# One layer step on one core: two plain FF blocks by tiles, the next weights ahead of an evaluation, staging kept, a late scaling

## The chip, the cores and the metric

The kernel runs on one NeuronCore of a Trainium2 chip. The metric is the device time of one execution in microseconds. Five engines have queues of their own and work each in its own order: TensorE (PE, matmuls and transposes), VectorE (DVE), ScalarE (ACT), GpSimd (POOL) and SyncE (SP, which issues the DMAs).

## What is computed

One layer of a streaming encoder, in fp32, for 512 prompt tokens and 8 sequences of 16 new tokens, each with 512 tokens in caches. Of the reference the parts that the change touches:

```python
def softmax_attend(q, k, v, bias):
    scale = q.shape[-1] ** -0.5
    s = jnp.einsum('bqhd,bkhd->bhqk', q, k).astype(jnp.float32) * scale + bias
    p = jax.nn.softmax(s, axis=-1).astype(v.dtype)
    return jnp.einsum('bhqk,bkhd->bqhd', p, v)
...
def layer_tail(x, ada, o_a, o_b, gates, w_o_a, w_o_b, w_out, g_norm_ffn, w_gate, w_up, w_down):
    shift1, scale1, gate1, shift2, scale2, gate2 = ada
    B, S = o_a.shape[:2]
    y_a = o_a.reshape(B, S, N_HEADS_A * V_DIM_A) @ w_o_a
    y_b = o_b.reshape(B, S, N_HEADS_B * HEAD_DIM_B) @ w_o_b
    x = x + gate1 * ((gates[:, :, 0] * y_a + gates[:, :, 1] * y_b) @ w_out)
    h = modulate(rmsnorm(x, g_norm_ffn), shift2, scale2)
    return x + gate2 * ((jax.nn.silu(h @ w_gate) * (h @ w_up)) @ w_down)
```

D_MODEL is 1024, D_FF 2816 (22 blocks of 128). Ahead of this stand the adaLN terms, an input projection, a latent attention (MLA) and a band attention, for the prompt and for the samples.

## The kernel before

Every fp32 operand is split in two parts of a shorter type, a high part (a cast on ACT, line 86) and a low part (a subtraction on DVE, line 87). A product is three matmuls into the same bank: high by high (L94), high by low of the activations (L95), low of the weights by high (L96). PSUM has two groups of four banks, tiles named mm and tr. The tokens are five tiles of 128: four of the prompt, one of the samples.

The program runs through stages. Ahead of 473 us: norms, projections, prompt attention. To 582: a loop over the 8 sample sequences. The softmax of the band scores divides by its sum with a `tensor_scalar` on DVE (L682); the probabilities are transposed on PE (L140) and multiplied by the cached values (L1003), and ACT copies the result to o2 (L1007). Then the latent values are projected up (L1070, to 585.74), and ACT copies them out (L1075) and casts them to `oh`, the high part of the attention outputs. Then w_o in four quarters of columns, to 657, w_out in two halves, to 714.7, and the feed-forward part.

Weights come by DMA into raw tiles of 128 x 1024 and are split from there. Up to the value projection the raw tiles are those of a pool wstA (3 of w_raw, 3 each of w_hi and w_lo, 1024 wide). Then that pool is closed, and a pool wops takes its place: 4 raw tiles and operands of 512 columns, 12 high (op_hi) and 11 low (op_lo).

The first two feed-forward blocks are plain: gate and up products of h with a block's weights, each over tiles 0 to 2 (384 columns) and tiles 3 and 4 (256). They run while the last tiles are still being made: h2_cols normalizes, transposes (xn to tr, L140) and modulates a tile's columns into hfull, and splits them into hB. Blocks 2 to 21 use seven products instead of eight halves, with sums of weight quarters made on POOL and DVE (`sums`, one buffer) and sums of h (hsum, hS). One of these, hB's fourth (fourth_sum), is made on DVE from hB and hS, and uses the buffer of `sums` too. The copies of partial products (u) that this needs are on ACT (L1293). Each engine's order is set by the order in which the program issues instructions, moved by a scheduler that runs ahead of the chip.

Of the kernel before, what the change touches and what calls it, by code (L numbers as in the profile page):

```python
# [17 lines left out]
P = 128  # L18
# [30 lines left out]
def layer_kernel(  # L49
# [117 lines left out]
    wa_cm = pool("wstA", side="right")  # L167
    wa = wa_cm.__enter__()

    raws = [3]  # L170

    def load_raw(src, shape, rows=P, given=P):
        n = shape[0] * shape[1]
        raw = wa.tile([P, 1024], F32, tag="w_raw", bufs=raws[0], name=nm("wraw"))[:rows, :n]
        rv = raw.rearrange("p (k n) -> p k n", k=shape[0])
        if given < rows:
            G.memset(raw, 0.0)
        nc.sync.dma_start(rv[:given], src)
        return raw, rv

    def load_kv_up(c0):
        raw = wa.tile([P, 1024], F32, tag="w_raw", bufs=raws[0], name=nm("wraw"))
        for k in range(2):
            nc.sync.dma_start(raw[:, k * 512:(k + 1) * 512].rearrange("p (h c) -> p h c", c=64),
                              wkv_v[:, k, :, c0:c0 + 64])
        return raw
# [491 lines left out]
    def softmax_rows(pl, src, nmax, w, dst, eng):  # L678
        sm = pl.tile([P, 1], F32, tag="sm", bufs=4, name=nm("sm"))
        S.activation(out=dst[:, :w], in_=src, func=AF.Exp, bias=nmax, accum_out=sm)  # L680
        V.reciprocal(sm, sm)
        eng.tensor_scalar(out=dst[:, :w], in0=dst[:, :w], scalar1=sm, scalar2=None, op0=ALU.mult)  # L682
# [153 lines left out]
    with pool("ework") as ew:  # L836
# [34 lines left out]
        def softmax(s, sc, mx):  # L871
            nmax = et([P, 1], "nmax", 4)
            V.tensor_reduce(out=nmax, in_=mx, op=ALU.max, axis=AX.X, negate=True)
            pr = et([P, KEYS], "Pr", 2)
            softmax_rows(ew, sc, nmax, KEYS, pr, V)
            pn = et([P, P], "Pn", 2)
            G.memset(pn, 0.0)
            G.tensor_copy(pn[:, s * DSEQ:(s + 1) * DSEQ], pr[:, PAST:])
            return pr, pn
# [101 lines left out]
        def band_softmax(st):  # L981
            sc, mx = et([P, KEYS], "S", 2), et([P, 2], "mx", 4)
            for hf in range(2):
                ks = slice(hf * KH, (hf + 1) * KH)
                V.tensor_tensor_reduce(out=sc[:, ks], in0=st["ps"][hf][:, :KH], in1=biasd[:, ::-1][:, ks], scale=1.0,
                                       scalar=-3e38, op0=ALU.add, op1=ALU.max, accum_out=mx[:, hf:hf + 1])
            st["P"] = softmax(st["s"], sc, mx)
# [6 lines left out]
        def band_values(st, half):  # L994
# [10 lines left out]
            if half:  # L1005
                st["o2"] = et([P, P], "o2", 2)
                S.copy(st["o2"], st["po"][:, :P])  # L1007
# [72 lines left out]
    wa_cm.__exit__(None, None, None)  # L1080

    wa = ctx.enter_context(pool("wops", side="right"))
    raws[0] = 4

    def operand(src, n=512):
        hi = wa.tile([P, 512], F32R, tag="op_hi", bufs=12, name=nm("ophi"))[:, :n]
        lo = wa.tile([P, 512], F32R, tag="op_lo", bufs=11, name=nm("oplo"))[:, :n]
        split(hi, lo, src)
        return hi, lo

    def operands(src, shape):
        raw = load_raw(src, shape)[0]
# [9 lines left out]
    def ada_rows(c0):  # L1102
        raw = wa.tile([P, 1024], F32, tag="w_raw", bufs=4, name=nm("wraw"))
# [4 lines left out]
    def gate_rows(c0, scale):  # L1108
# [3 lines left out]
        for c in range(2):  # L1112
            hi = wa.tile([P, 512], F32R, tag="op_hi", bufs=12, name=nm("ophi"))[0:AR, :]
            lo = wa.tile([P, 512], F32R, tag="op_lo", bufs=11, name=nm("oplo"))[0:AR, :]
# [116 lines left out]
    def ff_raw(fb):  # L1231
        cs_ = slice(fb * P, (fb + 1) * P)
        return [load_raw(v[:, :, cs_], [KD, P])[0] for v in (wg_v, wu_v)]
# [24 lines left out]
    def plain(bank, w, t0, t1):  # L1258
        for k in range(KD):
            ks = slice(k % 4 * P, (k % 4 + 1) * P)  # L1260
            h = [x[:, k // 4 * 2:k // 4 * 2 + 2, k % 4, t0 * 64:t1 * 64] for x in hB]
            mm3(bank[:, :(t1 - t0) * P].rearrange("p (a x) -> p a x", a=2), w[k // 4][0][:, ks], w[k // 4][1][:, ks],
                h[0], h[1], k == 0, k == KD - 1)

    w0 = operands_of(0)
    banks0 = [mm_tile() for _ in range(4)]
    plain(banks0[0], w0[0], 0, 3)
    h2_cols(4)
    plain(banks0[1], w0[1], 0, 3)
    plain(banks0[2], w0[0], 3, 5)  # L1270
    plain(banks0[3], w0[1], 3, 5)
# [11 lines left out]
    with pool("fwork") as fw:  # L1283
# [25 lines left out]
        def plain_block(banks0):  # L1309
            new_hidden()  # L1310
            for i, (t0, t1) in enumerate(((0, 3), (3, 5))):
                n = (t1 - t0) * P
                u = fw.tile([P, 512], F32, tag="tmp", bufs=2, name=nm("u"))[:, :n]
                S.activation(out=u, in_=banks0[2 * i][:, :n], func=AF.Silu)
                V.tensor_tensor(out=u, in0=banks0[2 * i + 1][:, :n], in1=u, op=ALU.mult)
# [22 lines left out]
        def ff_block(fb):  # L1338

            new_hidden()  # L1340
# [7 lines left out]
            G.tensor_tensor(out=s4, in0=a12, in1=a11, op=ALU.subtract)  # L1348
            pa, pb, pc = mm_tile(), tr_tile(), tr_tile()
            product(pa, o11, hB, 0)  # L1350
            u1 = part(pa, "u1", 2)
            product(pb, operand(s1), hS, 0)
# [38 lines left out]
        plain_block(banks0)  # L1391
        w1 = operands_of(1)
        banks1 = [tr_tile() for _ in range(4)]
        for i, (t0, t1) in enumerate(((0, 3), (3, 5))):
            for j in range(2):
                plain(banks1[2 * i + j], w1[j], t0, t1)
        plain_block(banks1)
        fourth_sum()
        ends = [0, 5, 10, 14, 18]
        for fb in range(2, NFF):  # L1400
            ff_block(fb)
# [60 lines left out]
```

## Time and profile before

| what | value |
|---|---|
| median of three runs | 1174.38 us (1174.12 to 1176.02) |
| the profiled execution | 1172.05 us, its span 1170.3 us |
| granted clock of TensorE, mean | 0.986 |
| PE busy | 1113.9 us, 95% of the span, 7187 matmuls |
| DVE, ACT, POOL busy | 737.1, 560.3, 214.1 us |

The span is what the trace covers; the 1.75 us around it are start and end. The times of the trace count from the start of the span.

### The profile page before, as it was taken

The page shows a single profiled execution, that of the slowest core. Times are in us where ns is not written, and L with a number is a line of the kernel's source. Part 1 is how long each engine was busy: PE and PEld are TensorE (multiplying, and loading weights), DVE is VectorE, ACT ScalarE, POOL GpSimd, SP SyncE. Part 2 cuts the span into 40 slices and gives each one's busy share as a digit, 9 for nine tenths or more (in the row PEclk, how much of TensorE's full clock was granted, in tenths as well). Part 3 has the DMA queues.
Part 4 walks back from the last instruction along what each step waited for, and adds up shares of the span by engine and source line. Part 5 has one row for each costly group of instructions (what it writes and reads, how often), then busy time and mean ns, then how long its engine had stood idle before and what let it go on. Part 6 is the DMA issues. An engine that isn't in the chain of part 4 may idle for free. (4 is left out here: it accounts for less than half of the span.)

```text
span 1170.3 us, 19416 instructions
## 1 busy us (share of the span) xinstructions
PE 1113.9 (95%) x7187; PEld 998.9 (85%) x7187; DVE 737.1 (63%) x1675; ACT 560.3 (48%) x1243; POOL 214.1 (18%) x289
## 2 busy tenths in 40 slices
PE   7898999999999999899879998899999999999998
PEld 6678988999897788798779987889899899899896
DVE  3688555747776654455456347786676677675744
ACT  4675533446665544466543246465155245253440
POOL 0010001010000000112012213243143233242320
PEclk9999999999999899999989998999999999999999
DMA  8832334587665445766496221034133223133112
GB/s 266 296 112 71 109 141 127 171 231 206 201 183 167 129 145 160 236 214 228 133 288 219 88 73 52 1 109 126 37 92 104 76 73 108 37 108 90 54 56 90
DMA packets 156425, 158.17 MB, mean 135 GB/s; under 512 B 24826, under 2 KB 115495, under 8 KB 156330
## 3 DMA queue, kind: packets, MB, share of 16 engines
q1 hardware_dynamic: 156330, 156.92, 43.5%
q8 instruction: 57, 0.93, 0.3%
q14 instruction: 38, 0.31, 0.1%
HBM read 136.59 MB, written 20.30 MB: 134 GB/s over the span
## 5 line engine op out<-in xcount | busy, mean ns | idle before, releaser
L86 ACT CAST ophi<-wraw 128x512 fp32r<-128x512 f32 (+1 forms) x188 | 113.7, 620 | 135.1 <-PE mm L96 52.8
L87 DVE TENSOR_TENSOR oplo<-wraw,ophi 128x512 fp32r<-128x512 f32 (+1 forms) x188 | 148.2, 805 | 37.5 <-ACT ophi L86 13.3
L94 PE MATMUL mm<-ophi,aT 128*128 128x512 f32 x220 | 87.1, 396 | 0.4 <-DVE u L1335 0.3
L95 PE MATMUL mm<-oplo,aT 128*128 128x512 f32 x220 | 86.9, 395 | 0.0
L96 PE MATMUL mm<-ophi,aTl 128*128 128x512 f32 x220 | 86.1, 395 | 0.0
L94 PE MATMUL mm<-hT_hi,whi 128*128 128x320 f32 x256 | 83.2, 325 | 1.5 <-ACT whi L86 1.5
L94 PE MATMUL mm<-whi,hT_hi 128*128 128x512 f32 (+3 forms) x240 | 79.5, 332 | 1.2 <-ACT jk L337 0.9
L96 PE MATMUL mm<-hT_hi,wlo 128*128 128x320 f32 x256 | 80.4, 314 | 0.0
L95 PE MATMUL mm<-hT_lo,whi 128*128 128x320 f32 x256 | 79.7, 311 | 0.0
L96 PE MATMUL mm<-whi,hT_lo 128*128 128x512 f32 (+3 forms) x240 | 79.4, 332 | 0.0
L95 PE MATMUL mm<-wlo,hT_hi 128*128 128x512 f32 (+3 forms) x240 | 79.3, 331 | 0.0
L94 PE MATMUL mm<-hB,ophi 128*128 128x320 f32 (+2 forms) x192 | 60.2, 316 | 4.6 <-ACT hB L86 4.6
L1386 DVE TENSOR_TENSOR tmp<-mm,gate 128x512 f32<-128x512 f32 x50 | 34.2, 688 | 43.4 <-PE mm L96 43.3
L95 PE MATMUL mm<-hB,ophi 128*128 128x320 f32 (+2 forms) x192 | 60.1, 314 | 0.5 <-DVE hB L87 0.5
L96 PE MATMUL mm<-hB,oplo 128*128 128x320 f32 (+2 forms) x192 | 59.9, 312 | 0.0
L94 PE MATMUL tr<-hB,ophi 128*128 128x320 f32 (+2 forms) x192 | 59.2, 309 | 0.0
L95 PE MATMUL tr<-hB,ophi 128*128 128x320 f32 (+2 forms) x192 | 59.2, 309 | 0.0
L87 DVE TENSOR_TENSOR wlo<-wraw,whi 128x1024 fp32r<-128x1024 f32 (+2 forms) x36 | 41.0, 1141 | 28.0 <-ACT whi L86 27.1
L96 PE MATMUL tr<-hB,oplo 128*128 128x320 f32 (+2 forms) x192 | 58.6, 309 | 0.0
L94 PEld LDWEIGHTS mm<-hT_hi,whi 128*128 128x128 f32 x256 | 48.7, 190 | 5.4 <-issue 2.1
L94 PE MATMUL mm<-hS,ophi 128*128 128x320 f32 x160 | 49.6, 310 | 3.3 <-ACT u L1293 3.3
L1344 POOL TENSOR_TENSOR sums<-wraw 128x512 f32<-128x512 f32 x20 | 28.3, 1416 | 130.3 <-DMA wraw<-in_w_up_dram 89.6
(374 smaller groups left out, 3272.8 us busy)
## 6 DMA issues: line engine op xcount, KB each, us to landing
adaw<-in_w_ada_dram SPq DMA_DIRECT2D x48, 512.0 KB
wraw<-in_w_in_dram SPq DMA_DIRECT2D x28, 512.0 KB
wraw<-in_w_gate_dram SPq DMA_DIRECT2D x22, 512.0 KB
wraw<-in_w_up_dram SPq DMA_DIRECT2D x22, 512.0 KB
wraw<-in_w_down_dram SPq DMA_DIRECT2D x20, 512.0 KB
lat<-in_cache_kv_latent_dram SPq DMA_DIRECT2D x16, 512.0 KB
wraw<-in_cache_band_v_dram SPq DMA_DIRECT2D x16, 512.0 KB
kn<-in_cache_band_k_dram SPq DMA_DIRECT2D x16, 512.0 KB
```

The source lines that it names most:

```text
L86: S.copy(hi, src)
L87: (eng or V).tensor_tensor(out=lo, in0=src, in1=f(hi), op=ALU.subtract)
L94: T.matmul(out, lh, rh, start=start, stop=False, skip_group_check=more)
L95: T.matmul(out, lh, rl, start=False, stop=False, skip_group_check=more)
L96: T.matmul(out, ll, rh, start=False, stop=stop, skip_group_check=more)
L1344: G.tensor_tensor(out=s1, in0=a21, in1=a22, op=ALU.add)
L1386: V.tensor_tensor(out=tmp, in0=banks[t], in1=gate2[t // 4][:, cc], op=ALU.mult)
```

## The change

Five edits. (1) The pool wstA stays open to the end. A smaller pool wops (1 raw tile, 6 high, 5 low) is opened beside it; operands are taken in turns of four, two as the halves of a w_hi/w_lo pair, two from wops, and every fourth raw tile comes from wops. The numbers stay 4 raw, 12 high, 11 low. (2) The plain blocks are taken together: tiles 0 and 1 of block 0 and of block 1 (256 columns, gate and up in one bank), then tiles 2 to 4 of both (384 columns). (3) The first steps of a seven-product block (loads, sums of quarters, the operands of the first two products) become a function of their own, ff_weights, and that of block 2 is called ahead of the evaluation of the plain blocks and of fourth_sum. (4) For the samples' band attention the probabilities are no longer scaled; the copy of o2 scales by 1/sum instead. (5) Weights that fill whole rows are loaded by a shorter function.

```diff
-    wa_cm = pool("wstA", side="right")
-    wa = wa_cm.__enter__()
-    raws = [3]
+    wa = ctx.enter_context(pool("wstA", side="right"))
...
-    def softmax_rows(pl, src, nmax, w, dst, eng):
+    def softmax_rows(pl, src, nmax, w, dst, eng, scaled=True):
         sm = pl.tile([P, 1], F32, tag="sm", bufs=4, name=nm("sm"))
         S.activation(out=dst[:, :w], in_=src, func=AF.Exp, bias=nmax, accum_out=sm)
         V.reciprocal(sm, sm)
+        if not scaled:
+            return sm
         eng.tensor_scalar(out=dst[:, :w], in0=dst[:, :w], scalar1=sm, scalar2=None, op0=ALU.mult)
...
-                S.copy(st["o2"], st["po"][:, :P])
+                S.activation(out=st["o2"], in_=st["po"][:, :P], func=AF.Copy, scale=st["sm"])
...
-    wa_cm.__exit__(None, None, None)
-
-    wa = ctx.enter_context(pool("wops", side="right"))
-    raws[0] = 4
+    wo2 = ctx.enter_context(pool("wops", side="right"))
+    turn, pair = [0, 0], [None, None]
+
+    def new_operand():
+        i, turn[0] = turn[0] % 4, turn[0] + 1
+        if i == 0:
+            pair[:] = [wa.tile([P, 1024], F32R, tag=tag, bufs=3, name=nm(tag)) for tag in ("w_hi", "w_lo")]
+        if i < 2:
+            return [o[:, i * 512:(i + 1) * 512] for o in pair]
+        return [wo2.tile([P, 512], F32R, tag=tag, bufs=n, name=nm(tag)) for tag, n in (("op_hi", 6), ("op_lo", 5))]
+
+    def new_raw():
+        i, turn[1] = turn[1] % 4, turn[1] + 1
+        return (wo2 if i == 2 else wa).tile([P, 1024], F32, tag="w_raw", bufs=1 if i == 2 else 3, name=nm("wraw"))
...
-    w0 = operands_of(0)
-    banks0 = [mm_tile() for _ in range(4)]
-    plain(banks0[0], w0[0], 0, 3)
-    h2_cols(4)
-    plain(banks0[1], w0[1], 0, 3)
-    plain(banks0[2], w0[0], 3, 5)
-    plain(banks0[3], w0[1], 3, 5)
+    w01 = [operands_of(0), operands_of(1)]
+    sums01 = []
+    for i in range(2):
+        bank = mm_tile()
+        sums01.append([[bank[:, 0:256], bank[:, 256:512]]])
+        for j in range(2):
+            plain(sums01[i][0][j], w01[i][j], 0, 2)
+        if i == 0:
+            h2_cols(4)
+    for i in range(2):
+        sums01[i].append([(tr_tile if i else mm_tile)()[:, :384] for _ in range(2)])
+        for j in range(2):
+            plain(sums01[i][1][j], w01[i][j], 2, 5)
...
-        def ff_block(fb):
-
-            new_hidden()
+        def ff_weights(fb):
             a11, a12, a21, a22 = quarters(fb)
             sums = fw.tile([P, 2, 512], F32, tag="sums", name=nm("sums"))
...
+            return a11, a12, a21, a22, s1, s4, o11, operand(s1)
+
+        def ff_block(fb, w):
+
+            a11, a12, a21, a22, s1, s4, o11, o1 = w
+            new_hidden()
...
-        plain_block(banks0)
-        w1 = operands_of(1)
-        banks1 = [tr_tile() for _ in range(4)]
-        for i, (t0, t1) in enumerate(((0, 3), (3, 5))):
-            for j in range(2):
-                plain(banks1[2 * i + j], w1[j], t0, t1)
-        plain_block(banks1)
+        first = ff_weights(2)
+        plain_block(sums01[0])
+        plain_block(sums01[1])
         fourth_sum()
         ends = [0, 5, 10, 14, 18]
         for fb in range(2, NFF):
-            ff_block(fb)
+            ff_block(fb, first if fb == 2 else ff_weights(fb))
```

What the change moves shows in the order of instructions on three engines. First SP's queue around the value projection (in_w_kv_up) and the first loads of w_o (in_w_o_a, in_w_o_b), before:

```order
L178 DMA wraw_7418<-in_cache_band_v_dram 128x2x512
L184 DMA wraw_7460<-in_w_kv_up_dram 128x8x64
L222 DMA ada_d<-adar_7404 105x512
L184 DMA wraw_7460<-in_w_kv_up_dram 128x8x64
L1147 DMA g_7569<-gate_d 128x640
L1147 DMA g_7571<-gate_d 128x640
L1147 DMA g_7639<-gate_d 128x640
L1147 DMA g_7641<-gate_d 128x640
L178 DMA wraw_7549<-in_w_o_a_dram 128x4x256
L178 DMA wraw_7559<-in_w_o_b_dram 128x4x256
```

And now:

```order
L175 DMA wraw_7400<-in_cache_band_v_dram 128x2x512
L175 DMA wraw_7410<-in_cache_band_v_dram 128x2x512
L181 DMA wraw_7452<-in_w_kv_up_dram 128x8x64
L219 DMA ada_d<-adar_7396 105x512
L181 DMA wraw_7452<-in_w_kv_up_dram 128x8x64
L1104 DMA wraw_7540<-in_w_o_a_dram 128x4x256
L1104 DMA wraw_7548<-in_w_o_b_dram 128x4x256
L1162 DMA g_7558<-gate_d 128x640
L1162 DMA g_7560<-gate_d 128x640
```

The two loads of w_o stood behind four loads of g, and stand ahead of them now; the loads of w_o use the raw slots that the band values (wraw_7400, wraw_7410) had.

Second PE in the plain blocks. The products of hB (hB_8262 or hB_8243 the high part, hB_8263 or hB_8244 the low part) with a block's weights stand around the transposes of the normalized tiles 3 and 4 (xn). Before, the transposes of tile 3 and then of tile 4, in block 0's products of tiles 0 to 2:

```order
L96 MATMUL mm_8832<-hB_8262,oplo_8821 128x384
L140 MATMUL tr_8768<-ident,xn_8741 128x128 x4
L140 MATMUL tr_8780<-ident,xn_8741 128x128 x4
L94 MATMUL mm_8832<-hB_8262,ophi_8820 128x384
...
L140 MATMUL tr_8860<-ident,xn_8810 128x128 x4
L140 MATMUL tr_8870<-ident,xn_8810 128x128 x4
L94 MATMUL mm_8833<-hB_8262,ophi_8824 128x384
```

Now, in the products of tiles 0 and 1 of block 1 (mm_8893); 70 matmuls stand ahead of the first, 14 between the two, and 12 behind the second. The last five rows begin the products of tiles 2 to 4:

```order
L94 MATMUL mm_8893<-hB_8243,op_hi_8811 128x256
L140 MATMUL tr_8741<-ident,xn_8714 128x128 x4
L140 MATMUL tr_8753<-ident,xn_8714 128x128 x4
L95 MATMUL mm_8893<-hB_8244,op_hi_8811 128x256
...
L96 MATMUL mm_8893<-hB_8243,w_lo_8816 128x256
L94 MATMUL mm_8942<-hB_8243,op_hi_8789 128x384
L94 MATMUL mm_8943<-hB_8243,w_hi_8797 128x384
L94 MATMUL tr_8992<-hB_8243,op_hi_8807 128x384
L94 MATMUL tr_8993<-hB_8243,w_hi_8815 128x384
L95 MATMUL mm_8942<-hB_8244,op_hi_8789 128x384
```

Before, 24 matmuls of 384 columns stood ahead of tile 3's transposes, and block 1's products of tiles 0 to 2 stood ahead of the first use of tiles 3 and 4; now tile 4 is needed right behind the 96 products of tiles 0 and 1.

Third DVE at the start of block 2. The tile t is that of fourth_sum (L1325 to L1327 before, L1346 to L1348 now), u and aTl belong to the evaluation of the plain blocks, and sums_... is block 2's sum of quarters. Before:

```order
L1315 TENSOR_TENSOR u_9110<-tr_9006,u_9110 128x256
L1326 TENSOR_TENSOR t_2006_9121<-t_2006_9121,hB_8263 128x640
L87 TENSOR_TENSOR aTl_9104<-u_9110,aT_9103 128x2x2x64
L1327 TENSOR_TENSOR t_2006_9121<-t_2006_9121,hS_8960 128x640
L87 TENSOR_TENSOR hB_8263<-t_2006_9121,hB_8262 128x640
L1345 TENSOR_TENSOR wraw_9131<-wraw_9129,wraw_9131 128x512
L87 TENSOR_TENSOR oplo_9160<-sums_9133,ophi_9159 128x512
```

And now:

```order
L87 TENSOR_TENSOR hS_9047<-hsum,hS_9046 128x1280 x3
L1336 TENSOR_TENSOR u_9077<-mm_8821,u_9077 128x256
L1364 TENSOR_TENSOR wraw_9060<-wraw_9058,wraw_9060 128x512
L87 TENSOR_TENSOR aTl_9076<-u_9077,aT_9075 128x2x2x64
L87 TENSOR_TENSOR op_lo_9072<-sums_9062,op_hi_9071 128x512
L87 TENSOR_TENSOR op_lo_9179<-wraw_9058,op_hi_9178 128x512
...
L87 TENSOR_TENSOR op_lo_9253<-wraw_9245,op_hi_9252 128x512
L1346 TENSOR_TENSOR t_1988_9099<-hB_8243,hS_9046 128x640
```

Block 2's weights (L1364 and the op_lo rows) stood behind the whole fourth sum, and stand ahead of its first row now.

## Rows read from the trace of the kernel before

**Rows 1.** Waits of PE: who waited for whom, us in total, times, longest.

```profile
PE mm L94 <- ACT ophi L86: 6.7, 1, 6.7
...
PE mm L94 <- ACT u L1293: 3.3, 2, 2.0
PE tr L140 <- DVE Pr L682: 2.7, 6, 0.9
```

**Rows 2.** Timeline of PE: start, us, what; idle time before it and releaser.

```profile
592.47 0.63 PE L94 MATMUL mm<-oh,ophi 128*128 128x320 f32 x1 [6.73 <-ACT ophi L86]
...
719.36 1.01 PE L94 MATMUL mm<-hB,ophi 128*128 128x384 f32 x2 [4.64 <-ACT hB L86]
...
758.52 0.63 PE L94 MATMUL tr<-hS,ophi 128*128 128x320 f32 x1 [4.54 <-ACT ophi L86]
...
790.71 0.41 PE L94 MATMUL mm<-hS,ophi 128*128 128x320 f32 x1 [2.02 <-ACT u L1293]
```

**Rows 3.** Windows: length, busy us of PE, PEld, DVE, ACT, POOL; clock, DMA share, GB/s.

```profile
585.74:587.74 2.00, 0.00 (x0) 0.00 (x0) 1.86 (x5) 1.91 (x7) 0.00 (x0) 1.00 0.73 256
587.74:592.47 4.73, 0.00 (x1) 0.00 (x1) 1.72 (x5) 3.25 (x10) 0.00 (x0) 0.51 1.00 292
592.47:598.20 5.73, 5.73 (x22) 5.50 (x22) 3.53 (x6) 2.74 (x5) 0.00 (x0) 0.51 1.03 336
...
719.36:724.40 5.04, 4.54 (x13) 4.03 (x14) 3.42 (x10) 3.57 (x6) 2.04 (x3) 0.50 0.04 13
...
758.50:761.90 3.40, 3.38 (x12) 3.15 (x13) 1.58 (x3) 0.79 (x2) 2.99 (x2) 0.50 0.00 0
...
790.70:840.00 49.30, 49.29 (x265) 43.83 (x266) 31.98 (x48) 18.81 (x38) 13.29 (x12) 1.00 0.32 97
```

**Rows 4.** Timeline of SP's queue: the first two loads of w_o.

```profile
585.81 0.39 SPq L178 DMA_DIRECT2D wraw<-in_w_o_a_dram  x1
586.24 0.51 SPq L178 DMA_DIRECT2D wraw<-in_w_o_b_dram  x1
```

**Rows 5.** Timeline of ACT between the samples and w_o, and in w_o.

```profile
582.19 4.42 ACT L86 CAST oh<-oT 128x320 fp32r<-128x320 f32 x12
586.63 2.20 ACT L1075 COPY oT<-mm 64x128 f32<-64x128 f32 x8
...
591.80 1.14 ACT L86 CAST ophi<-wraw 128x512 fp32r<-128x512 f32 x2 [1.40 <-DMA wraw<-in_w_o_a_dram]
...
602.64 1.14 ACT L86 CAST ophi<-wraw 128x512 fp32r<-128x512 f32 x2 [4.92 <-DMA wraw<-in_w_o_b_dram]
```

**Rows 6.** Timeline of PE: last band values, tile 3's transposes, the plain blocks' pace.

```profile
578.15 0.64 PE L1003 MATMUL mm<-wraw,PTb 128*32 128x128 f32 x16 [1.83 <-DMA wraw<-in_cache_band_v_dram]
...
726.43 1.03 PE L140 MATMUL tr<-ident,xn 128*128 128x128 f32 x8
...
743.77 0.34 PE L94 MATMUL tr<-hB,ophi 128*128 128x384 f32 x1
...
746.38 0.28 PE L94 MATMUL tr<-hB,ophi 128*128 128x256 f32 x1
...
752.06 0.31 PE L94 MATMUL mm<-hB,ophi 128*128 128x320 f32 x1
```

**Rows 7.** Timeline of DVE: low parts of tiles 1 and 4.

```profile
710.79 2.37 DVE L87 TENSOR_TENSOR hB<-hfull,hB 128x512 fp32r<-128x512 f32 x2
...
734.73 2.22 DVE L87 TENSOR_TENSOR hB<-hfull,hB 128x512 fp32r<-128x512 f32 x2
```

**Rows 8.** Timeline of ACT: a modulation, tile 4's xn and its cast.

```profile
717.25 0.46 ACT L1211 ACTIVATE hfull<-tr,B,A 128x128 f32<-128x128 f32 x1 [0.74 <-DVE rs L108]
...
723.16 1.15 ACT L1195 ACTIVATE xn<-x,rs 128x1024 f32<-128x1024 f32 x1 [0.81 <-DVE rs L111]
...
734.08 1.22 ACT L86 CAST hB<-hfull 128x512 fp32r<-128x512 f32 x2 [3.58 <-DVE hfull L1220]
```

**Rows 9.** Timeline of POOL: block 2's first sum.

```profile
756.56 1.26 POOL L1344 TENSOR_TENSOR sums<-wraw 128x512 f32<-128x512 f32 x1 [19.01 <-DVE hB L87]
```

**Rows 10.** The copies of o2 (ns min/median/max), and one scaling of band probabilities (timeline).

```profile
L1007 ACT COPY o<-mm x8: 242/246/267, 494.3 to 579.1; 128x128 f32<-128x128 f32 x8
...
521.55 0.49 DVE L682 TENSOR_SCALAR Pr<-Pr,sm 128x528 f32<-128x528 f32 x1
```

## What the change is predicted to do

> **What bounds the kernel now.** Begin with the waits of TensorE (PE). The page's first part has it busy for 95% of the span, so what can still be won is the rest, 56 us, and the time that PE works at half clock. [rows 1] name whom it waits for after the prompt attention; two waits on an ACT cast and one on hB stand out. The timeline [rows 2] says where they are: 6.73 us ahead of the first w_o product (to 592.47), 4.64 us ahead of the first plain FF product (to 719.36), 4.54 us ahead of the second product of FF block 2 (to 758.52), and 2.02 us in the next block, to 790.71. The windows [rows 3] add a second price. PE is idle through 585.74:587.74 at granted clock 1.00; in 587.74:592.47 the clock is 0.51, and it stays there for the first 22 matmuls of w_o (592.47:598.20); after the other two stalls it is 0.50 for about 5 and 3.4 us. That is 1.2 instead of 2.4 GHz. The last window (790.70:840) shows the opposite: PE 49.29 of 49.30 us busy at 1.00. There PE waits for nothing, so an edit there can only cost. The change is therefore worth what it takes from those three stalls and the two small ones on L1293.
>
> **Staging kept: the start of w_o.** In the rows of SP's queue in the order above, the loads of w_o_a and w_o_b stand behind four loads of g; in time, w_o_a is issued at 585.81 and w_o_b 0.43 us later [rows 4], when the old pool has been given up. The cast of w_o_a starts at 591.80, 6.0 us after the issue [rows 5], and PE starts 0.67 us behind that. In the new order both loads stand ahead of the g loads and need only the w_raw slots of the last two band-value tiles. Their last readers are the matmuls at 578.15 [rows 6], so w_o_a can be issued at about 578.6 and, at the same 6.0 us, is there at 584.6. ACT isn't free then: the 12 casts of oh run from 582.19 to 586.61, and the new order puts two of the eight copies of L1075 (2.20 us for eight, 0.55 for two) ahead of the two w_hi casts [rows 5]. So the cast starts at 587.2 and PE at 587.2 + 0.67 = 587.85 in place of 592.47: **-4.6 us**; 2.1 us of idle time remain. The clock comes on top. 22 matmuls took 5.73 us there. Full clock shows in block 2's first product: it starts at 752.06 and PE falls idle at 758.52 - 4.54 = 753.98, so its 12 matmuls of 320 columns (0.31 us for the last) go at 1.61/11 = 0.146 each. 22 of them take 3.2: 2.5 us more if the clock doesn't fall. By [rows 3] it fell about 2.0 us into the old gap, just where the new one ends; after the 2.02 us that ended at 790.71 it hadn't fallen, as the last window shows. A toss-up: I take half, -1.3. Term -5.9, from -3 (a part of the loads late) to -7.1.
>
> What could be late next is the second w_o_b load, whose cast waited until 602.64 in a stretch in which the DMA engines were full (share 1.00 and 1.03 in [rows 3]). The first quarter of w_o is 96 matmuls, 14.0 us, which from 587.85 ends at 601.9. At the old time the cast would let PE go at 602.64 + 0.67 = 603.3 [rows 5], 1.4 us late; but the new queue issues that load ahead of the x loads, so I cost it at nothing.
>
> **Plain blocks by tiles.** Before, the first products take tiles 0 to 2 and wait for tile 2's hB. Now they take tiles 0 and 1, whose low parts end at 713.16 [rows 7], before PE is out of w_out (719.36 - 4.64 = 714.72). The stall of 4.64 goes. The matmuls stay 96 of 256 and 96 of 384 columns; by [rows 6], 15 of 384 columns take 746.38 - 743.77 = 2.61 us (0.174 each), 48 of 256 columns 752.06 - 746.38 = 5.68 (0.118). From 714.7 the 70 matmuls ahead of tile 3's transposes (second excerpt of the order) take 8.3 us: these go at 723.0 instead of 726.43, 3.4 us sooner; tile 4's xn ends at 724.31 [rows 8], in time for its own transposes 14 matmuls later (725.7). Tiles 0 and 1 of both blocks end at 714.7 + 96 x 0.118 + 16 transposes (1.6) = 727.6.
>
> Now the stall comes back in another place. Tiles 2 to 4 need tile 4. Its cast to hB started 734.08 - 726.43 = 7.65 us after tile 3's transposes, and its low part, from 734.73, was half done 1.1 us on [rows 7, 8]. That chain is DVE's and ACT's and only moves with the transposes, 3.4 us: the first half of the high part is there at 731.3, of the low part at 732.4. Before, tile 4 cost nothing, since block 1's tiles 0 to 2 stood in between; now PE idles 3.7 us from 727.6, does the four matmuls that the high part allows (rows L94 at the excerpt's end) and idles 0.4 us more. The remaining 92 matmuls of 384 columns take 16.0: end at 748.4 instead of 752.06, **-3.7** at full clock. But a gap of 4 us is like the old ones, after which the clock was half for 5 us [rows 3]; that gives back 2.5. Between -1.2 and -3.7 I take -2.2, nearer to the fall that the rows of such gaps show.
>
> **Block 2's weights ahead.** POOL's first sum of block 2 starts at 756.56, after 19 us idle [rows 9]: its tile "sums" has one buffer, which the fourth sum of hB holds. PE waits for the cast of it, 4.54 us. With the weights issued first, the sum takes that buffer first and needs only the raw tiles; in the third excerpt the low part made of it (op_lo<-sums) stands ahead of every row of the fourth sum. POOL is free from 756.56 - 19.01 = 737.6. The fourth sum now comes later on DVE, but its first reader is the last product of block 2, some 100 matmuls on. Gone: 4.54; the 12 matmuls after it, 3.38 us at clock 0.50 for 1.76 (12 x 0.146), 1.6; and the two waits on L1293, 3.3 in all [rows 1], which I read as ACT catching up behind the same knot. In all -9.4. Some of the last comes back, since block 2 starts earlier while gate rows and block 3's casts want the same engines: **-8.0**, from -4.5 (the stall alone) to -9.4.
>
> **Late scaling, and the cost of pairs.** Eight DVE rows of 0.49 us leave [rows 10]. PE's waits for L682 [rows 1], 2.7 us in six, stand ahead of transposes of the latent attention's Pr, whose scaling stays; so no gain is sure, 2.7 at most. The copy of o2 gets a pointer as scale: 0.246 us [rows 10], against 0.46 us for an ACTIVATE of the same shape with two such operands [rows 8]; eight times 0.21 is 1.7 us at most, and the transpose of o that reads it comes about 5 us later. I take +0.5 for the moved exps. The Trainium skill, "ScalarE: Activation LUTs", section "What ACT_TABLE_LOAD costs", speaks against this edit: each pointer operand adds about 93 ns to an ACTIVATE, by which the sum would be 0.74 us worse if nothing hid it; rows of this case agree with about 0.1 us for one.
>
> For blocks 3 to 21 operands come in pairs of halves, freed together. PE has no gap there to win, so I take +1, from 0 to +4 (0.2 us in each of 20 blocks).
>
> **Sum.** -5.9 - 2.2 - 8.0 + 0.5 + 1.0 = -14.6. The profiled execution took 1172.05 us (span 1170.3), 0.2% below the median of 1174.38; against the median the sum gives **1159.8**.
>
> **Rivals.**
> - *The stalls move.* Tile 4 is as late as worked out with the clock down, of block 2 only the 4.54 goes, w_o keeps its half clock, and 2.5 us come back on ACT: -4.6 - 1.2 - 4.5 + 2.5 = -7.8, 1166.6. For it speaks that each stall is the end of a chain through ACT and DVE that goes on behind it; against it, that in 758.50:761.90 DVE is busy for 1.58 and ACT for 0.79 of 3.40 us.
> - *No fall of the clock.* Both gaps left are short enough: -4.6 - 2.5 - 3.7 - 9.4 + 0.5 = -19.7, 1154.7. The 2.02 us gap speaks for it, those of over 4 us against.
> - *The loads of w_o don't come earlier* (the change doesn't do that part), for instance because a slot waits for a cast queued behind oh: 1159.8 + 5.9 = 1165.7. The new order of SP's queue speaks against it.
> - *Slower: pairs hold up the part copies.* ACT works in order. A cast that waits for a pair still in use would hold the copy of a part (L1293) behind it, and PE waits for that copy before it adds to the same bank. The price for one such wait is in the trace: 2.0 us for the longest, 1.3 for the other [rows 1]. At 1.3 in each of 20 blocks it is 26 us: 1174.4 - 15.6 + 26 = 1184.8. It decides from 15.6/20 = 0.78 us per block. Against it: the number of high and low operands is as before (12 and 11), and PE's window of 49 us has no such gap.
>
> **How the numbers follow.** The forecast 55%, stalls move 18%, no fall of the clock 12%, loads not earlier 5%, pairs hold up the copies 6%, the last 4% for gains that cancel. 1154 to 1168 takes in the first four. Faster by over 0.2% (what a measurement of this kernel can tell from no change): the first four, 0.90; same 0.04; slower 0.06.
>
> **What would show it.** w_o_a issued near 579 and PE's first w_o matmul near 587.9; no wait at 714.7 but one of 3 to 4 us near 727, released by hB, and the clock behind it; no POOL sum between the plain blocks' end and the second product of block 2; full PE in blocks 3 to 21. The forecast is wrong if PE's wait for L1293 shows up in many blocks, or if the gap at tile 4 is gone or doubled.

## The result, and the profile after

The changed kernel takes 1161.51 us (median of 4 runs, 1156.91 to 1166.06), the kernel before 1174.47 beside it: ratio 0.9893, interval 0.9867 to 0.992, faster by 13.0 us. Measured a second time, as after_again, it came to 0.9894 (0.987 to 0.9918). The profiled execution is the longest of the four, 1166.06 us with a span of 1164.3. Two executions in a slow state, one of `both` at 1559.15 us and one of the kernel before at 6174.19, are left out of all that follows.

The page's first parts: busy time of the engines, and the granted clock of PE in 40 slices of 29.1 us.

```profile
PE 1122.0 (96%) x7187; PEld 1003.6 (86%) x7187; DVE 736.3 (63%) x1667; ACT 555.2 (48%) x1243; POOL 213.5 (18%) x289
...
PEclk9999999999999989999989999899999999999999
```

PE's idle time is 42 us in place of 56, while its busy time grew by 8 with the same 7187 matmuls: it worked longer at the low clock. The slice with an 8 ahead of the middle (407 to 436 us) is the prompt attention, code that the change doesn't touch. The windows (columns as in [rows 3]) show another fall there, which the slices round away. First the kernel before, at the same place:

```profile
370.00:390.00 20.00, 18.30 (x117) 16.13 (x116) 12.69 (x42) 10.52 (x28) 1.58 (x3) 1.00 0.41 120
```

And now, with the places of the old stalls:

```profile
370.00:390.00 20.00, 18.00 (x97) 16.11 (x97) 10.27 (x32) 7.83 (x20) 0.40 (x1) 0.83 0.51 146
592.00:595.00 3.00, 3.00 (x18) 3.00 (x18) 2.76 (x8) 2.94 (x9) 0.00 (x0) 0.60 0.87 288
...
602.00:605.00 3.00, 3.00 (x14) 3.00 (x14) 2.04 (x5) 1.75 (x4) 0.00 (x0) 0.56 0.94 239
...
735.20:740.00 4.80, 4.80 (x15) 4.80 (x16) 4.80 (x4) 4.10 (x4) 2.78 (x3) 0.50 0.00 0
...
795.00:840.00 45.00, 45.00 (x224) 38.45 (x223) 26.13 (x39) 10.91 (x23) 9.05 (x8) 1.00 0.29 88
```

Further on in this stage it falls in both, to 0.68 in 400:410 before and 0.66 in 410:420 here. The first 2790 matmuls are the same in both, in the same order; the 1601st starts at 285.2 us in both profiles, the 2401st at 413.8 before and 419.4 here. The samples' first product of band keys (kT) starts 5.8 us later here (483.90 against 478.15). So the whole time of one execution says little about a single edit, and the stretches below are compared one by one.

The waits of PE from 470 us on (as in [rows 1]):

```profile
PE mm L94 <- ACT hB L86: 3.5, 1, 3.5
PE tr L140 <- DMA kn<-in_cache_band_k_dram: 1.8, 2, 1.0
PE tr L225 <- DMA wraw<-ada_d: 1.6, 1, 1.6
PE mm L1003 <- DMA wraw<-in_cache_band_v_dram: 1.5, 1, 1.5
...
PE mm L1070 <- DMA wraw<-in_w_kv_up_dram: 1.0, 1, 1.0
PE mm L94 <- ACT u L1315: 0.7, 1, 0.7
```

Of the waits of [rows 2] the ones of 6.73 and 4.54 us are gone; that on hB is 3.5 us and stands elsewhere; two on loads are new. The timeline of PE says where:

```profile
588.59 0.46 PE L1070 MATMUL mm<-olatT,wraw 128*128 128x128 f32 x2 [0.63 <-ACT oT L1017]
590.03 5.24 PE L1070 MATMUL mm<-olatT,wraw 128*128 128x128 f32 x30 [0.98 <-DMA wraw<-in_w_kv_up_dram]
...
595.03 0.39 PE L94 MATMUL mm<-oh,w_hi 128*128 128x320 f32 x1
...
599.80 0.36 PE L225 MATMUL tr<-sel,wraw 106*128 106x9 f32 x2 [1.58 <-DMA wraw<-ada_d]
...
735.20 0.69 PE L94 MATMUL mm<-hB,op_hi 128*128 128x384 f32 x1 [3.50 <-ACT hB L86]
...
756.46 0.31 PE L94 MATMUL tr<-hS,op_hi 128*128 128x320 f32 x1
```

And the queue of SP, for [rows 4], and POOL, for [rows 9]:

```profile
583.00 1.07 SPq L181 DMA_DIRECT2D wraw<-in_w_kv_up_dram  x1
584.16 1.14 SPq L1104 DMA_DIRECT2D wraw<-in_w_o_a_dram  x1
585.41 2.45 SPq L1104 DMA_DIRECT2D wraw<-in_w_o_b_dram  x1
589.14 1.76 SPq L1162 DMA_DIRECT2D g<-gate_d  x4
595.35 0.34 SPq L1120 DMA_DIRECT2D wraw<-ada_d  x1
```

```profile
742.26 1.29 POOL L1363 TENSOR_TENSOR sums<-wraw 128x512 f32<-128x512 f32 x1 [4.29 <-issue]
```

w_o_a is issued ahead of the value projection, w_o follows it without a gap, and block 2's sum is made 12 us ahead of block 2. But PE waits 0.98 us for the second half of w_kv_up, with w_o_a issued right behind it at 584.16. That w_o_a delays it isn't shown: tiles_only (below), where no load of w_o is issued before the value projection has ended, has the same wait of 1.0 us.

The adaLN rows (ada_d) are issued at 595.35 only, and PE waits 1.58 us for them. Their raw tile is the third in turn, the one of the new pool wops, and 595.35 is 0.08 us behind the end of the value projection (590.03 + 5.24). In the kernel before it is w_o_a that goes out 0.07 us behind that end (585.74, and 585.81 in [rows 4]). In each of the fourteen profiles the first load into a raw tile of wops goes out 0.07 or 0.08 us behind the end of the value projection. So the raw tiles of the pool that stays open are filled early, and the one of the pool that is opened late still waits, as all four did before.

For the comparisons the end of the program is cut in three by first rows of PE in the timeline: from the value projection (L1070) to the first matmul of w_out, from there to block 2's first matmul (320 columns), from there to PE's last row. In us, one profile each:

| kernel | to w_out | to block 2 | to the end |
|---|---|---|---|
| before | 75.5 | 94.6 | 413.6 |
| after; after_again | 72.7; 70.8 | 93.4; 92.3 | 405.0; 406.8 |
| staging_only | 71.2 | 95.2 | 413.7 |
| tiles_only | 76.7 | 92.7 | 413.2 |
| weights_only | 73.9 | 94.9 | 407.3 |
| scaling_only | 75.2 | 94.8 | 414.2 |
| sums_free | 73.0 | 95.8 | 409.1 |
| three_stretches | 71.5 | 92.3 | 406.2 |
| ada_later | 70.0 | 92.3 | 405.9 |
| both | 70.0 | 92.3 | 406.2 |
| mixed | 71.8 | 89.6 | 407.6 |
| mixed_ada | 70.4 | 89.7 | 407.6 |
| mixed_ada_noscale | 70.4 | 89.6 | 407.7 |

Kernels that share the code of a stretch differ by up to 3.7 us in the first (73.0 to 76.7 without the staging), by 1.2 in the second and about 2 in the third.

### The profile page after: what moved, and what is told of

Same layout as the page of the kernel before. It is cut to its first block, busy times and chain, and to the rows that moved or that the text cites. A ratio compares the mean times of both kernels' runs of the same rounds, so it can differ in the third digit from the quotient of the medians.

```text
span 1164.3 us, 19347 instructions
## 1 busy us (share of the span) xinstructions
PE 1122.0 (96%) x7187; PEld 1003.6 (86%) x7187; DVE 736.3 (63%) x1667; ACT 555.2 (48%) x1243; POOL 213.5 (18%) x289
## 4 chain that ended last, share of the span: by engine, by line
PE 82%; DMA 8%; DVE 6%; ACT 2%; issue 1%; SPq 1%; POOL 1%; DVEq 0%; POOLq 0%; ACTq 0%
PE mm L94 21%; PE mm L96 20%; PE mm L95 20%; PE tr L140 6%; PE tr L94 3%; PE tr L96 3%; PE tr L95 3%; DMA wraw<-in_w_in_dram 2%; PE mm L213 2%; DMA adaw<-in_w_ada_dram 1%; PE mm L952 1%; DVE op_lo L87 1%; DMA kn<-in_cache_band_k_dram 1%; PE mm L977 1%; PE mm L804 1%
## 5 line engine op out<-in xcount | busy, mean ns | idle before, releaser
L87 DVE TENSOR_TENSOR op_lo<-wraw,op_hi 128x512 fp32r<-128x512 f32 x94 | 78.1, 835 | 18.5 <-PE mm L96 10.5
L86 ACT CAST w_hi<-wraw 128x512 fp32r<-128x512 f32 (+2 forms) x95 | 56.1, 624 | 66.7 <-PE mm L96 42.4
L87 DVE TENSOR_TENSOR w_lo<-wraw,w_hi 128x512 fp32r<-128x512 f32 (+2 forms) x95 | 76.9, 835 | 13.6 <-ACT w_hi L86 13.0
L86 ACT CAST op_hi<-wraw 128x512 fp32r<-128x512 f32 x94 | 57.1, 620 | 34.4 <-PE mm L96 9.5
L96 PEld LDWEIGHTS mm<-hT_hi,wlo 128*128 128x128 f32 x256 | 50.0, 195 | 0.9 <-DVE kTl L87 0.7
L95 PEld LDWEIGHTS mm<-hT_lo,whi 128*128 128x128 f32 x256 | 50.1, 196 | 0.3
L94 PEld LDWEIGHTS mm<-whi,hT_hi 128*128 128x128 f32 x240 | 45.2, 188 | 5.1 <-ACT jk L334 1.3
L95 PEld LDWEIGHTS mm<-wlo,hT_hi 128*128 128x128 f32 x240 | 45.2, 188 | 3.4
L96 PEld LDWEIGHTS mm<-whi,hT_lo 128*128 128x128 f32 x240 | 45.1, 188 | 3.3
L94 PE MATMUL mm<-w_hi,aT 128*128 128x512 f32 x115 | 45.6, 397 | 0.7 <-DVE u L1356 0.6
```

The costliest lines, as they stand in the source:

```text
L86: S.copy(hi, src)
L87: (eng or V).tensor_tensor(out=lo, in0=src, in1=f(hi), op=ALU.subtract)
L94: T.matmul(out, lh, rh, start=start, stop=False, skip_group_check=more)
L95: T.matmul(out, lh, rl, start=False, stop=False, skip_group_check=more)
L96: T.matmul(out, ll, rh, start=False, stop=stop, skip_group_check=more)
```

## The experiments

**Each edit alone.** Four kernels, each the kernel before with one edit. The staging (the pool wstA isn't closed; new_operand and new_raw as in the change; the shorter load function, the fifth edit, is in this run too and was not run by itself):

```diff
-    wa_cm.__exit__(None, None, None)
-    wa = ctx.enter_context(pool("wops", side="right"))
-    raws[0] = 4
+    wo2 = ctx.enter_context(pool("wops", side="right"))
```

> The kernel before with the first edit alone: the pool of raw tiles stays open, operands in pairs. Theory T (each edit has a term of its own, as the two traces give it): from the value projection's first matmul to w_out's first, 75.5 us in the kernel before and 72.7 in the changed one, so about 72.7 here, with a new wait of PE for a load of the adaLN rows (some 1.6 us) and one for the load of w_kv_up (some 1 us); nothing else moves: 1171.5 us, ratio 0.9975. Rival R1 (the forecast's term of -5.9 holds and the profiled run of the changed kernel was unlucky): 69.6 us there, 1168.5, ratio 0.995. Rival R2 (pairs hold up copies of parts in the seven-product blocks): the last 356 us grow by several us, no gain in sum.

The ratio is 0.998 (0.9962 to 0.9999), the stretch to w_out 71.2 us. PE starts w_o 5.97 us behind the first matmul of the value projection, where the forecast had 5.95 (587.85 less 581.90, its start in the kernel before), and the two longest waits of this stretch are

```profile
PE mm L94 <- ACT w_hi L86: 2.0, 1, 2.0
PE mm L94 <- DVE t L1169: 1.1, 1, 1.1
```

The 2.0 us are the idle time that was forecast to remain; behind them the clock is 0.56 (593.30:596). The gain of 4.4 us lies between T and R1, but it is taken against one profile: against the five without the staging (73.0 to 76.7) it is 1.8 to 5.5. The stretch of blocks 2 to 21 is as before (413.7), so R2 falls: no cost of pairs shows. The expected new waits for loads aren't in this profile, so they come in some executions and not in others.

The plain blocks by tiles:

```diff
+    w01 = [operands_of(0), operands_of(1)]
...
+            plain(sums01[i][0][j], w01[i][j], 0, 2)
...
+            plain(sums01[i][1][j], w01[i][j], 2, 5)
```

> The kernel before with the plain blocks taken together by tiles alone. Theory T: PE starts behind w_out without a wait, waits some 3.5 us for tile 4's hB, at half clock behind it; from w_out's end to block 2's first matmul 36.3 us in place of 37.3; in sum -1 us, 1173.4, ratio 0.999. Rival R3 (the edit leans on block 2's weights): what it wins ahead of block 2 is lost there, since the sum of quarters still waits behind the fourth sum on DVE: the wait of 4.5 us for block 2's second operand grows by as much, 0 in sum or slower.

Ratio 0.9977 (0.9955 to 0.9999); to block 2 92.7 us, 2.0 less than before, and the stretch behind it as before (413.2). The waits of PE from 710 us on:

```profile
PE tr L94 <- ACT ophi L86: 4.1, 1, 4.1
PE mm L94 <- ACT hB L86: 3.5, 1, 3.5
PE mm L94 <- ACT u L1300: 3.0, 2, 1.9
```

Block 2's wait is 4.1 us, not longer by what was won: R3 falls.

Block 2's weights ahead (ff_weights as in the change):

```diff
+        first = ff_weights(2)
         plain_block(banks1)
         fourth_sum()
...
-            ff_block(fb)
+            ff_block(fb, first if fb == 2 else ff_weights(fb))
```

> The kernel before with block 2's weights (loads, sums of quarters, two operands) issued ahead of the evaluation of the second plain block and of the fourth sum. Theory T: no wait of 4.5 us ahead of block 2's second product, no half clock behind it, the two waits for the copies of L1293 shrink: from block 2's first matmul to the first down product 49 us in place of 58: -8.9, 1165.5, ratio 0.9924. Rival R3 (the edits lean on each other): the operands of block 1 fill the staging, block 2's come as late as before; less than -4, ratio over 0.9966.

Ratio 0.994 (0.9916 to 0.9963); from block 2 to the end 407.3 us, 6.3 less. So the edit stands by itself and is the largest, and its R3 falls. It is short of the 8.9 of T by about what PE still waits, most of it for copies of parts (waits of PE in 750:800):

```profile
PE mm L94 <- ACT u L1293: 1.7, 2, 1.0
PE tr L96 <- DVE oplo L87: 0.8, 1, 0.8
PE tr L94 <- ACT u L1293: 0.3, 1, 0.3
```

The late scaling:

```diff
-            st["P"] = softmax(st["s"], sc, mx)
+            *st["P"], st["sm"] = softmax(st["s"], sc, mx, False)
...
-                S.copy(st["o2"], st["po"][:, :P])
+                S.activation(out=st["o2"], in_=st["po"][:, :P], func=AF.Copy, scale=st["sm"])
```

> The kernel before with the late scaling of the band probabilities alone. Theory T: eight DVE rows of 0.49 us go from slack, the copy of o2 gets 0.12 us longer off the path: the sample loop stays at 110 us, ratio 1.000 within 0.001. Rival R4 (DVE's scaling is on the path of the latent attention's transposes): the waits of PE for Pr, 2.7 us in six, go: 1171.7, ratio 0.9977.

Ratio 1.0008 (0.999 to 1.0027). Four waits of 0.39 us for Pr are gone, and nothing is won; a period of the sample loop grew. It is the distance between the first products of band keys (kT) of two sequences: 11.36 to 11.37 us in the middle of the loop in each of the profiles without this edit, 11.67 to 11.70 in each with it. The timeline of PE at such a place, in the kernel before:

```profile
527.75 1.08 PE L1003 MATMUL mm<-wraw,PTb 128*32 128x128 f32 x32
...
528.86 1.09 PE L978 MATMUL mm<-kT,qbd 128*32 128x264 f32 x16
530.34 0.63 PE L140 MATMUL tr<-ident,Pr 128*128 128x128 f32 x4 [0.39 <-DVE Pr L682]
```

And here:

```profile
526.83 0.65 PE L1005 MATMUL mm<-wraw,PTb 128*32 128x128 f32 x16
...
527.50 1.54 PE L980 MATMUL mm<-kT,qbd 128*32 128x264 f32 x16
528.98 0.44 PE L140 MATMUL tr<-ident,Pr 128*128 128x128 f32 x2
```

From the products of kT to the transposes of Pr it is 1.48 us here (528.98 - 527.50). In the kernel before it is the same 1.48 (528.86 to 530.34), of which 0.39 is the wait. The wait was idle time all the same: there the 16 products start within 0.70 us, four at a time, here within 1.16, in fours, threes and singles. What the wait gave up, the products took. So R4 misses, and T on the loop: five periods are longer by 0.31 us, 1.5 in all.

What differs is PE's order: with the edit the first half of the band values (L1005) stands between transposes of kn, and only the second half (526.83) behind them; before, both stood there in one piece (527.75). Pn's transpose stands earlier, too. Counted from each matmul's start to the next one's, one such period differs in the transposes of kn (1.76 us before, 1.91 here), the band values (0.90 and 1.04) and those of Pr (0.82 and 0.85), and by 0.01 us at most in any other tile. So the 0.31 us are paid where PE changes between transposes of kn and band values, twice more than before; Pn's new place costs nothing.

**Sum of the parts.** By stretches, -4.4 - 2.0 - 6.3 = -12.7, and with the 1.5 of the loop -11.2. By the whole times it is -0.2, -0.2, -0.6 and +0.1%, about -11 us. Measured are -13.0. The four intervals, each some 2 us to either side, and that of the changed kernel leave this open to 5 us or so: within that the edits add, and a smaller gain or loss of one by another can't be seen.

**The knot at block 2.** Was it the buffer, or the order in which the work is issued? The kernel before, its program in the old order, but the fourth sum in four pieces in another tile:

```diff
-            for k in range(0, 4, 2):
-                k2 = slice(k, k + 2)
-                t4 = fw.tile([P, 2 * 512], F32, tag="sums", name=nm("t4"))[:, :2 * HALF]
+            for k in range(4):
+                t4 = fw.tile([P, 512], F32, tag="tmp", bufs=2, name=nm("t4"))[:, :HALF]
```

> The kernel before, with its order of issue, but the fourth sum of hB made in four pieces in the tile tmp, so that it no longer holds the one buffer of the sums of quarters. Theory T (the buffer is the knot): POOL makes block 2's sum without the 19 us of idle time, the wait of 4.5 us and the half clock behind it go, from block 2's first matmul to the end 407 us as in weights_only, against 413.6: ratio about 0.994. Rival R7 (the order in which the program issues the work is the knot, the buffer a symptom): the sum still comes behind the plain blocks' evaluation and the fourth sum; 413 us, ratio 1.000.

Ratio 0.9961 (0.994 to 0.9982), 409.1 us from block 2 on, and POOL's first sum:

```profile
742.58 1.30 POOL L1342 TENSOR_TENSOR sums<-wraw 128x512 f32<-128x512 f32 x1 [4.29 <-PE mm L96]
```

It stands 14 us earlier than in [rows 9], with the program in the old order, and the wait of 4.5 us is gone. So the buffer was the knot, and R7 falls. But the order on the chip isn't the old one: with the buffer free, DVE's first row of the fourth sum stands behind block 2's rows, 12.5 us later than before (in weights_only it starts at 752.11). In the kernel before, and here:

```profile
741.74 0.83 DVE L1325 TENSOR_TENSOR t<-hB,hS 128x640 f32<-128x640 f32 x1
```

```profile
754.25 0.48 DVE L1323 TENSOR_TENSOR t<-hB,hS 128x320 f32<-128x320 f32 x1
```

The run shows that the buffer held back block 2's sum. It doesn't show what a free buffer would give if DVE kept its old order.

About 2 us of weights_only are missing. PE's waits are 0.4 us longer in sum here: 2.3 for copies of parts, 0.9 for the cast of the fourth sum (ACT hB). The clock makes up most of the rest: behind the longest of them, 1.8 us, it is 0.50 in 775:777, and in weights_only 1.00 from 743 us on.

**The changed kernel again, and two repairs.** A second profile, and then the plain blocks in three stretches:

```diff
-        sums01[i].append([(tr_tile if i else mm_tile)()[:, :384] for _ in range(2)])
...
-            plain(sums01[i][1][j], w01[i][j], 2, 5)
+            plain(sums01[i][1][j], w01[i][j], 2, 4)
...
+            plain(sums01[i][2][j], w01[i][j], 4, 5)
```

> The changed kernel once more, beside the kernels of this call. Theory T: a ratio near 0.989, with single times spread over some 9 us, because PE's clock falls in some executions behind waits of 1.4 to 2 us in the prompt attention, which the change doesn't touch; the waits themselves as in the first profile. Rival: the spread comes from the stages that changed; then the stretch from the value projection to w_out or from w_out to block 2 differs by over 2 us between the two profiles.

> The changed kernel with the plain blocks in three stretches: tiles 0 and 1, tiles 2 and 3, tile 4 (256, 256 and 128 columns), so that tile 4's chain lies behind 96 matmuls of tiles 2 and 3. Theory T: the wait of 3.5 us and about 2 us of half clock go, and 96 matmuls more of 128 columns cost little: from w_out's end to block 2 31 us in place of 36.3, -5 against the changed kernel. Rival R5 (short matmuls are bound by their weight loads): 128 columns take as long as 256, 0.118 us each, 96 of them 11.4 in place of 5.7, and the gain is eaten: 0 within 1 us.

after_again: the single times lie 5.6 us apart (1158.58 to 1164.2), in place of 9. The second and third stretches agree with the first profile to 1.2 and 1.8 us, the first to 1.9, just under the 2 us of the rival. T misses on the waits: those for w_kv_up and the adaLN rows aren't there, and one of 2.0 us for w_hi is, ahead of w_o. The two profiles reach the value projection 6.7 and 6.2 us later than the kernel before's does, and of that 5.8 and 5.3 us lie ahead of the samples' first product of kT; T holds for that part. three_stretches: 0.9877 (0.9852 to 0.9902), the wait on hB is gone, the clock is 1.00 from 714.4 to 749.5, and yet the stretch to block 2 is 92.3 us, as in the changed kernel. The timeline of PE has the first and last matmul of tile 4, 96 of 128 columns, and block 2's first:

```profile
738.86 0.23 PE L94 MATMUL mm<-hB,op_hi 128*128 128x128 f32 x1
...
749.42 0.28 PE L96 MATMUL mm<-hB,w_lo 128*128 128x128 f32 x1
749.53 0.36 PE L94 MATMUL mm<-hB,op_hi 128*128 128x320 f32 x1
```

(749.53 - 738.86)/96 = 0.111 us each, against 0.118 for 256 columns [rows 6]: half the columns at nearly the same price. So R5 holds as to the price, and the gain of 5 us is paid for 96 more matmuls. That the weight loads set the price isn't shown.

The adaLN rows a quarter of w_o later:

```diff
-            if bg == 0:
+            if bg == 1:
                 ada_shift(B2, ada_cols(ada_rows(3 * DM), 8))
-            elif bg == 1:
-                ada_scale(A2, ada_cols(ada_rows(4 * DM), 8), gffn)
             elif bg == 2:
+                ada_scale(A2, ada_cols(ada_rows(4 * DM), 8), gffn)
                 gate1 = gate_rows(2 * DM, 0.5)
```

> The changed kernel with the adaLN rows of the second norm one quarter of w_o later in the program, so that their transposes stand behind the second quarter and their raw tile isn't asked for in the first. Theory T: PE's wait of 1.6 us for the load of these rows goes, and with it the half clock behind it: -3 us against the changed kernel between w_o's first matmul and w_out's. Rival R6: the DMA engines are full there, and the wait moves to the second quarter's weights or to the gate rows ahead of w_out: 0 within 1 us.

0.9875 (0.9848 to 0.9902), median 1157.44; to w_out 70.0 us. No wait for ada_d is left in 578:655, and PE's clock is 1.00 in all windows from the value projection to w_out. R6 falls in this profile. But after_again has no such wait either, in the old order: against it the gain in the stretch is 0.8 us, against the first profile 2.7. The wait comes and goes (0.7 in three_stretches, 0.9 in mixed). From w_o's first matmul to w_out's the four profiles with this edit take 63.8 to 64.5 us, the four of the changed order without it 64.8 to 66.3.

> The two edits of three_stretches and ada_later together. Theory T: the gains add, -8 against the changed kernel, ratio about 0.982. Rivals R5 and R6 as there.

0.9897 (0.987 to 0.9924), so T misses: it is 70.0 and 92.3 us, the one gain stays, and the other, eaten as above, stays eaten. The whole time doesn't show the first.

**Half the price for the cover.** Block 0 in three stretches, block 1 in two:

```diff
+    for i, n, t0, t1 in ((0, 1, 2, 4), (1, 1, 2, 5), (0, 2, 4, 5)):
         for j in range(2):
-            plain(sums01[i][1][j], w01[i][j], 2, 5)
+            plain(sums01[i][n][j], w01[i][j], t0, t1)
```

> The changed kernel with block 0's products in three stretches (tiles 0 and 1, 2 and 3, 4) and block 1's in two (0 and 1, 2 to 4), so that only 48 matmuls more are needed to cover tile 4's chain. Theory T (128-column matmuls cost 0.11 us each, as three_stretches shows: 96 more, 5.2 us for 10.7 us of work, paid for the wait of 3.5 and the half clock): here half of that price; from w_out's first matmul to block 2 some 89.6 us in place of 92.3, -2.7 against the changed kernel, ratio about 0.987. Rival R8 (two tiles more are too short a cover): part of the wait comes back, 91 us or more.

0.9877 (0.9854 to 0.99); to block 2 89.6 us, as forecast, without a wait, so R8 falls. But from there to the end it is 407.6, over 1 us more than in three_stretches or ada_later. The waits of PE in 715:800:

```profile
PE mm L94 <- ACT u L1319: 2.0, 2, 1.0
PE tr L94 <- ACT u L1319: 0.5, 1, 0.5
```

PE comes sooner to block 2, ACT doesn't, and the copies of parts take a part back (2.5 us in all, 1.1 in three_stretches).

> The edits of mixed and of ada_later together. Theory T: both gains stay, -2.7 and about -2 against the changed kernel: w_o's first matmul to w_out 63.8 us, w_out to block 2 89.6 us, ratio about 0.985. Rival: the whole time can't show it because PE's clock falls in the prompt attention in some executions; then the two stretches are shorter and the ratio is within 0.002 of the changed kernel's.

0.9877 (0.9857 to 0.9897), to block 2 89.7 us as expected; the stretch to w_out is 70.4, and its w_o takes 64.5 us instead of 63.8. The clock fell there (below), and PE waits 0.6 us for the copy of the gate rows (ACT, L1140) ahead of w_out, as R6 had it; how the 0.7 us divides between these stays open, since the next kernel takes 64.5 too, at full clock, with 0.8 us for that copy. The rival holds for the whole time.

> mixed_ada with the late scaling taken back: the band probabilities are scaled by DVE again, o2 is copied plainly. Theory T (late scaling costs time on PE, through the order in which the scheduler puts transposes and band values): five of the seven periods of the sample loop, 11.69 us in each profile with the edit and 11.37 in each without, are 11.37 again, with PE's wait of 0.39 us for the scaling back in each; from the loop's first product of band keys to the value projection 103.0 to 103.9 us in place of 104.5; -1.0 us to -1.5 against mixed_ada in the profile. Rival R9 (the longer period is a matter of DVE's or the DMAs' load in the loop): with the other edits in place it stays 11.69. The whole time, whose spread is several us, can't tell a difference of 1 us.

The edit is scaling_only's, taken back. 0.9868 (0.9841 to 0.9895); the middle periods are 11.36 and 11.37 us again, with the waits of 0.39, so R9 falls. Since only the scaling is taken back, this shows that the edit makes the longer period. The sum of 103 to 104 us missed: 105.4, as the clock fell to 0.50 behind the loop's last wait of 1.9 us. ada_later, mixed, mixed_ada and this one have overlapping intervals; each is below the changed kernel's 0.9894, none by more than they can tell.

## Why the prediction was right

Forecast 1159.8 us, measured 1161.51; the sum -14.6, measured -13.0.

- *w_o, -5.9.* The mechanism and the start were right: w_o begins 5.96 us behind the value projection's first matmul in after_again, 6.44 in the first profile, for the 5.95 worked out. The size was off: the stretch shrank by 2.8 and 4.8 us, by 4.4 alone. Two terms failed. The forecast asked only whether w_o's own loads would be late. That the adaLN rows get the one raw tile that still waits for the end of the value projection wasn't in it (1.58 us in the first profile, none in after_again). And the clock's half of 1.3 us didn't come in these profiles: behind the gap of 2 us it fell at once in staging_only and some us later, behind further small gaps, in after_again. In ada_later and in the run called both, where the gap ahead of w_o is 1.2 us, it didn't fall, and the stretch is 70.0, 5.5 less than before.
- *Plain blocks, -2.2.* Measured -1.2 and -2.4, alone -2.0. The wait at tile 4 was forecast as 3.7 and 0.4 us, at 13 us behind w_out; it is 3.5 at 13.1, with no second part of note, and the clock behind it is 0.50, as taken. That the same stall only comes back shorter was the core of this step.
- *Block 2, -8.0, with +1 for the steady blocks.* -8.6 and -6.9 against -7.0; alone -6.3. The wait and its half clock went; of the two waits on the copies of parts one of 0.66 stayed. sums_free shows that the buffer held back the sum, as the step said. The +1 for pairs measured nothing (413.7 in staging_only against 413.6).
- *Late scaling, +0.5.* Small as said, for a reason that wasn't named: PE's order. Five periods cost 1.5 us, and the rest of the loop gives a part back: from the first product of kT to the value projection it is 104.5 to 104.8 us in seven profiles with the edit, 103.5 to 103.9 in four without it (in three more the clock fell at the loop's end). Four of the six waits that I gave to the latent attention's Pr were the band's, so that reading was wrong too; it cost nothing, since the new order took what they gave.
- *Rivals.* Stalls that move came true in part (w_o's and tile 4's), the slower case not at all.
- *Luck.* w_o alone was short by 1.1 to 3.1 us, and single runs of the changed kernel lie 9 us apart. That the median comes within 1.7 us of the forecast is in part luck; that the gain is near 13 us, with its largest part at block 2, isn't.

## What to carry to other kernels

A load that is issued earlier takes its place in the turn of tiles: list all that it passes, and look which of the tiles in turn are free early and which still wait for the end of a stage. Where a stall ends in a buffer with one copy, look who else takes that buffer; freeing it was worth most here, and a change of order was only one way to do it. A stall that is to be covered by splitting work has a price per instruction, which can be as large as the stall.

## What the runs showed of the hardware

PE's clock after a wait of about 2 us is not settled by the wait. The windows of two kernels, first mixed_ada, then mixed_ada_noscale, each with a wait for band values and one ahead of w_o, and what followed:

```profile
579.40:581.00 1.60, 0.00 (x1) 0.01 (x1) 0.00 (x0) 0.68 (x2) 0.00 (x0) 1.00 0.81 257
581.00:582.50 1.50, 1.50 (x30) 1.30 (x31) 0.00 (x0) 0.37 (x1) 0.00 (x0) 1.00 1.09 282
588.70:590.70 2.00, 0.01 (x1) 0.00 (x0) 1.75 (x6) 1.94 (x7) 0.00 (x0) 1.00 0.81 302
590.70:594.00 3.30, 3.29 (x11) 2.92 (x12) 1.76 (x3) 3.16 (x10) 0.00 (x0) 0.53 1.03 318
```

```profile
577.00:579.20 2.20, 0.33 (x7) 0.09 (x9) 0.00 (x0) 0.75 (x2) 0.00 (x0) 1.00 0.87 279
579.20:582.00 2.80, 2.80 (x32) 2.42 (x33) 0.00 (x0) 0.27 (x1) 0.00 (x0) 0.58 0.83 211
588.30:590.50 2.20, 0.08 (x2) 0.05 (x1) 1.96 (x6) 2.14 (x7) 0.00 (x0) 1.00 0.80 280
590.50:594.00 3.50, 2.81 (x14) 2.02 (x14) 1.96 (x4) 3.37 (x10) 0.00 (x0) 1.00 0.97 310
```

Behind 2.0 us of idle time the clock is 0.53 in the one and, behind 2.2, 1.00 in the other; at the place before it is the other way about. The same happens in the prompt attention: behind 1.70 us of idle time it is 1.00 in the kernel before (373:375) and behind 2.00 it is 0.50 in the changed one (376:378); behind 1.46 and 1.35 us it fell in both (0.55 in 403.4:405, 0.51 in 410:414).

Runs of one kernel differ by 2 to 14 us. The clock is a part of that, and not shown to be all of it: the waits of the prompt attention differ too (near 309 us from 1.2 to 3.6 in the fourteen profiles), and two runs of after_again with mean clocks of 0.985 and 0.986 take 1164.2 and 1160.49 us.

In a dense stream a matmul of 128 columns costs 0.111 us, one of 256 0.118, one of 384 0.174 [rows 6]. The copy of o2 with a pointer as scale takes 0.367 us in the changed kernel (median of eight), 0.121 more than the plain one [rows 10]; the Trainium skill, "ScalarE: Activation LUTs", section "What ACT_TABLE_LOAD costs", has about 0.093 for such an operand, and the measured number decides. The 0.121 holds a change of instruction too, from COPY to ACTIVATE.
